# Strassen products for the FFN up projections of a two-layer decoder step, and a down projection in groups of four tiles

## The chip, the core and the metric

The kernel runs on one core of a Trainium2 chip. The metric is device time in microseconds: the median of three runs was 2255.38 us (2253.37 to 2259.19). One more execution was profiled; its time was 2256.28 us and the span of its trace, from the first to the last instruction, 2254.5 us. Engines are named as in the profile: PE (matmul), PEld (the weight load before each matmul), DVE (VectorE), ACT (ScalarE), POOL (GpSimd) and SP (whose queue issues the weight DMAs).

## The reference

One step of two layers over 512 prompt tokens and 32 sample tokens (544 columns in all), model width 1024. A layer has a half-step FFN, a mixing part (state-space heads and windowed attention), a second half-step FFN and a gated input embedding:

```
def _swiglu(x, w1, w3, w2):
    return (jax.nn.silu(x @ w1) * (x @ w3)) @ w2
...
    h = h + (0.5 * _swiglu(_rmsnorm(h, lp['g_ffn1']), lp['w1_a'], lp['w3_a'], lp['w2_a'])).astype(hd)
    ... mixing ...
    h = h + (0.5 * _swiglu(_rmsnorm(h, lp['g_ffn2']), lp['w1_b'], lp['w3_b'], lp['w2_b'])).astype(hd)
    gate = jax.nn.sigmoid(_rmsnorm(h, lp['g_ple']) @ lp['w_ple_gate'])
    h = h + (gate * (pe.astype(hd) @ lp['w_ple_proj'])).astype(hd)
```

`w1` and `w3` (the up projections) are 1024 x 2752, `w2` (the down projection) 2752 x 1024, all float32. The FFN runs four times in the step.

## The kernel before

**Numbers in two halves.** Each float32 operand is split into a rounded part and the rest, `wh` and `wl` for weights, `XH` and `XL` for activations. A product takes three matmuls for each 128 x 128 weight block: `wh` with `XH`, `wh` with `XL`, `wl` with `XH` (`terms3`, L103). A matmul has 128 x 128 weights and 272 columns, half of the 544, so that a pair of PSUM banks holds one output tile (`gemm`, L107).

**Weights.** `load_piece` (L89) takes a raw buffer of 8 blocks (128 x 1024 elements), issues its DMA on SP (L92), makes `wh` by a copy on ACT (L95) and `wl` by a subtraction on DVE (L96). `raw`, `wh` and `wl` have three buffers each (pool `wp`, L45).

**FFN** (L219 to L297). The 2752 hidden units are 21 tiles of 128 and a remainder of 64. For each tile j, `xtile` computes `w1`'s product (8 blocks x 3 terms x 2 halves = 48 matmuls), `act` (L229) takes it out of PSUM, scaled by the norm's factor `Rb` (two DVE instructions, L127), and forms SiLU by a tanh on ACT (L233), a DVE step (L234) and a POOL multiplication (L235); then `w3`'s product takes 48 matmuls, is multiplied in (L271, two DVE instructions) and kept as `UH` (ACT, L272) and `UL` (DVE, L273). After 11 tiles the down projection over these 11 is done for each of the eight 128-row tiles m of `h` and added into `h` (L296); then the other ten tiles and the remainder follow with their own down projection. One down tile over both parts is 130 matmuls. In the second FFN of a layer, `early` (L267) issues `ple_prep` (L1012: two DMAs, ten transposes, four ACT copies, four DVE subtractions) after the second tile, for the embedding stage that follows.

**What sets the order.** The kernel is written as one program; a planner at build time gives each engine its list of instructions. It prefers what stands earlier in the program, but puts a later instruction first where it expects the earlier one not to be ready, and it reuses a buffer of a pool only behind the last reader of what was in it. On the chip each engine works through its list strictly in order. Pools that are opened later lie over the memory of closed ones and wait tile by tile (`reuse_waits="tile"`).

**Elsewhere.** `mix` (L300) uses `piece` and `load_piece` for `w_in` and `w_out`; a loop written by hand (`fill`) mixes these products with attention and scan work. `Norm` (L130) scales and splits `h` into `XH` and `XL` and sums squares, with POOL adding (L151) and PE summing over rows (L156) and spreading the result (L168, L170).

Of the kernel before, what the change touches and what calls it, by code (L numbers as in the profile page):

```python
# [9 lines left out]
F32 = mybir.dt.float32  # L10
F32R = mybir.dt.float32r
# [10 lines left out]
NS = NB * NT  # L22
N = NP + NS
HN = N // 2
KD = DM // 128
DFF = 2752
NJ = DFF // 128
# [11 lines left out]
def hymba_step(ctx: ExitStack, tc: tile.TileContext, I, O):  # L39
# [2 lines left out]

    base = ctx.enter_context(tc.tile_pool(name="base", bufs=1))
    prm_p = ctx.enter_context(tc.tile_pool(name="prm", bufs=2))
    wp = ctx.enter_context(tc.tile_pool(name="wp", bufs=3))  # L45
    nrm = ctx.enter_context(tc.tile_pool(name="nrm", bufs=2))
    psp = ctx.enter_context(tc.tile_pool(name="ps", bufs=8, space=PSUM))

# [37 lines left out]
    V.memset(mhalf, -0.5)  # L86


    def load_piece(parts, nk):  # L89
        raw = wp.tile([128, KD, 128], F32, tag="raw", name="raw")  # L90
        for dst, src in parts:
            nc.sync.dma_start(out=dst(raw), in_=src)  # L92
        wh = wp.tile([128, KD, 128], F32R, tag="wh", name="wh")
        wl = wp.tile([128, KD, 128], F32R, tag="wl", name="wl")
        A.copy(wh[:, 0:nk, :], raw[:, 0:nk, :])  # L95
        V.tensor_sub(wl[:, 0:nk, :], raw[:, 0:nk, :], wh[:, 0:nk, :].bitcast(F32))  # L96
        return wh, wl

    def piece(w, r0, c0, nk):
        src = w[r0:r0 + nk * 128, c0:c0 + 128].rearrange("(k p) m -> p k m", p=128)  # L100
        return load_piece([(lambda t: t[:, 0:nk, :], src)], nk)

    def terms3(wp_, k, xh, xl):  # L103
        wh, wl = wp_
        return [(wh[:, k, :], xh), (wh[:, k, :], xl), (wl[:, k, :], xh)]

    def gemm(groups):  # L107
# [105 lines left out]
                 dtb=b4[:, 1, :], sink=b4[:, 2, :], dsk=dsk, srow=srow)  # L213


    HA = 11
    NWK = 6

    def ffn(g, w1, w3, w2, begun=None, early=None):  # L219
        if begun:  # L220
            first, norm = begun
        else:
            first = (piece(w1, 0, 0, KD), piece(w3, 0, 0, KD))
            norm = Norm(g)
        with tc.tile_pool(name="ffn", bufs=2, reuse_waits="tile") as fp:
            UH = fp.tile([128, HA, N], F32R, tag="UH", name="UH", bufs=1)
            UL = fp.tile([128, HA, N], F32R, tag="UL", name="UL", bufs=1)

            def act(ps1, np_=128):  # L229
                t1 = fp.tile([128, N], F32, tag="t1", name="t1")  # L230
                evac_r(t1, ps1, np_)
                th = fp.tile([128, N], F32, tag="th", name="th")
                A.activation(th[0:np_, :], t1[0:np_, :], AF.Tanh, scale=0.5)  # L233
                V.scalar_tensor_tensor(th[0:np_, :], th[0:np_, :], 1.0, t1[0:np_, :], op0=ALU.add, op1=ALU.mult)  # L234
                G.tensor_tensor(th[0:np_, :], th[0:np_, :], Rb[0:np_, :], op=ALU.mult)  # L235
                return th

            for j0, j1, rem in ((0, HA, False), (HA, NJ, True)):
                for j in range(j0, j1):
                    if rem and j == j1 - 1:  # L240
                        c0 = NJ * 128
                        ps = xgemm(load_piece(
                            [(lambda t: t[:, :, 0:FREM], w1[:, c0:DFF].rearrange("(k p) m -> p k m", p=128)),
                             (lambda t: t[:, :, FREM:128], w3[:, c0:DFF].rearrange("(k p) m -> p k m", p=128))], KD))
                        b = fp.tile([64, N], F32, tag="u64", name="b64", bufs=1)
                        for a in range(2):
                            A.copy(b[:, HALF[a]], ps[a][64:128, 0:HN])
                        s = act(ps, 64)
                        u = fp.tile([128, N], F32, tag="t1", name="ur")
                        V.tensor_tensor(u[0:64, :], b, s[0:64, :], op=ALU.mult)  # L250
                        A.copy(UH[0:64, j1 - j0, :], u[0:64, :])
                        V.tensor_sub(UH[64:128, j1 - j0, :], u[0:64, :], UH[0:64, j1 - j0, :].bitcast(F32))
                    if j == 0:
                        p1 = xgemm(first[0])
                        if not begun:
                            norm.sums()
                        p3 = xgemm(first[1])
                        if begun:
                            norm.sums()
                            pn = xtile(w1, 128)  # L260
                        norm.spread()
                        s = act(p1)
                    else:
                        p1 = pn if begun and j == 1 else xtile(w1, j * 128)
                        s = act(p1)
                        p3 = xtile(w3, j * 128)
                    if j == 1 and early:  # L267
                        early()
                    u = fp.tile([128, N], F32, tag="t1", name="u")
                    for a in range(2):  # L270
                        V.tensor_tensor(u[:, HALF[a]], p3[a][:, 0:HN], s[:, HALF[a]], op=ALU.mult)  # L271
                    A.copy(UH[:, j - j0, :], u)  # L272
                    V.tensor_sub(UL[:, j - j0, :], u, UH[:, j - j0, :].bitcast(F32))  # L273
                nk = j1 - j0
                for m in range(KD):
                    groups = []
                    k0 = 0
                    cuts = [6, nk - 6]
                    for ci, kn in enumerate(cuts):
                        r0 = (j0 + k0) * 128  # L280
                        cs = slice(m * 128, (m + 1) * 128)
                        parts = [(lambda t, kn=kn: t[:, 0:kn, :],
                                  w2[r0:r0 + kn * 128, cs].rearrange("(k p) m -> p k m", p=128))]
                        last = rem and ci == len(cuts) - 1
                        if last:
                            for a in range(2):
                                parts.append((lambda t, kn=kn, a=a: t[a * 64:(a + 1) * 64, kn, :], w2[NJ * 128:DFF, cs]))
                        p = load_piece(parts, kn + int(last))
                        terms = [t for k in range(kn) for t in terms3(p, k, UH[:, k0 + k, :], UL[:, k0 + k, :])]
                        if last:  # L290
                            terms += [(p[0][:, kn, :], UH[:, nk, :]), (p[1][:, kn, :], UH[:, nk, :])]
                        groups.append(terms)
                        k0 += kn
                    ps = gemm(groups)
                    for a in range(2):
                        V.scalar_tensor_tensor(h[:, m, HALF[a]], ps[a][:, 0:HN], 0.25, h[:, m, HALF[a]],  # L296
                                               op0=ALU.mult, op1=ALU.add)  # L297


    def mix(l, P):  # L300
# [3 lines left out]
        with tc.tile_pool(name="mx", bufs=1, reuse_waits="tile") as mp:  # L304
# [271 lines left out]
            rows = mp.tile([64, 168], F32R, tag="rows", name="rows")  # L576

            def step_load():
                raw = wp.tile([128, KD, 128], F32, tag="raw", name="raw")
                nc.sync.dma_start(out=raw, in_=w_in[:, C_DT:C_DT + 128].rearrange("(k p) m -> p k m", p=128))  # L580
                wh = wp.tile([128, KD, 128], F32R, tag="wh", name="wh")
                A.copy(wh, raw)
                V.tensor_sub(wh[:, :, NH:2 * NH], raw[:, :, 0:NH], wh[:, :, 0:NH].bitcast(F32))
                return wh

            def step_gemm(wh):
                ps = gemm([[t for k in range(KD) for t in ((wh[:, k, :], XH[:, k, :]), (wh[:, k, :], XL[:, k, :]))]])
                S["dtf"] = dtf = wk()[:, 0:640]
                evac_r(dtf, ps, 2 * NH)
                G.tensor_copy(dtf[0:2 * NH, NP + NS:640].rearrange("p (a s) -> p a s", s=NS), bc(dtf[0:2 * NH, NP:NP + NS], 1, 3))  # L590
# [290 lines left out]
            def wo_load(part, m):  # L881
                cs = slice(m * 128, (m + 1) * 128)
                if part == 1:
                    return piece(w_out, 0, m * 128, 4)
                return load_piece([(lambda t, a=a: t[a * 64:(a + 1) * 64, 0:4, :],
                                    w_out[512 + a * 256:512 + (a + 1) * 256, cs].rearrange("(j p) m -> p j m", p=64))
                                   for a in range(2)], 4)

# [212 lines left out]
    for l in range(DEPTH):  # L1101
# [5 lines left out]
            V.tensor_copy(selr, sel[:, NH:NH + 4])  # L1107
        mix_params(l, P)
        mix(l, P)
        with tc.tile_pool(name="ple", bufs=2, reuse_waits="tile") as lp:  # L1110
            E = []
            ffn(P["g2"], I["w1_b"][l], I["w3_b"][l], I["w2_b"][l], early=lambda: E.extend(ple_prep(l, lp)))
            Pn = params(l + 1) if l + 1 < DEPTH else None
            ple(l, P, lp, E, l == DEPTH - 1)
        P = Pn
# [64 lines left out]
```

## Time and profile before

| what | value |
| --- | --- |
| median of three runs | 2255.38 us |
| profiled execution | 2256.28 us, of which the span is 2254.5 us |
| mean granted PE clock | 0.989 |
| ACT busy | 699.2 us (31%) |
| POOL busy | 379.8 us (17%) |
| bytes moved by DMA | 197.74 MB, mean 88 GB/s |
| weight loads of 512 KB for `w1`, `w3` | 84 for each of `in_w_a` and `in_w_b` |

Times are in microseconds unless marked ns. In the views by windows, each engine has its busy time in that stretch and, in brackets, its instructions; then come the PE clock as a share of full speed, the share of DMA and GB/s. In the timelines a row has its start, its length, engine, line, operation, output and inputs, and in square brackets the idle time before it with what ended that. In the view of groups by form a row has the total busy time, then the mean of one in ns. Matmuls are pipelined: one lasts about 290 ns in the record, but the next begins after less than half of that, so PE time is counted from start to start. Rows on DVE and ACT overlap their neighbours a little in the same way.

### The profile page before, as it was taken

Reading aid. Unit: us, or ns where it says so; the run is one execution under the profiler, and the core shown is the slowest. Engines: PE = TensorE matmul, PEld = TensorE weight load, DVE = VectorE, ACT = ScalarE, POOL = GpSimd, SP = SyncE. Lnnn points to the kernel's source line nnn. Section 1 sums busy time; section 2 is a strip of 40 time slices with the busy share of each in tenths; the row PEclk is TensorE's granted clock in tenths of the full one; section 3 lists DMA queues with packets and bytes.
Section 4 is the critical chain, followed back from the end, with each engine's and each line's share of the span. In section 5 each row is a group of like instructions: output and inputs, shape, how many; then the busy total and the mean of one; then the engine's idle time right before and its main releaser. Section 6 shows DMA issues by size and latency. Waiting matters only on the chain.

```text
span 2254.5 us, 41580 instructions
## 1 busy us (share of the span) xinstructions
PE 2221.2 (99%) x17666; PEld 2186.0 (97%) x17666; DVE 1161.2 (52%) x2064; ACT 699.2 (31%) x1126; POOL 379.8 (17%) x361
## 2 busy tenths in 40 slices
PE   8999999999999999999999999999999999999999
PEld 8999999989899999999999999999898999999998
DVE  5443444489774434444554334444988644344444
ACT  4221223344342222233432222233443432122333
POOL 3000111233521100101111001112334211001110
PEclk9999999999999999999999999999998999999999
DMA  6323332322243323322333233233123432233223
GB/s 174 99 74 105 85 82 84 92 68 57 65 133 83 88 77 98 93 72 88 96 86 91 72 102 93 72 100 77 50 62 85 125 85 82 79 104 87 78 80 87
DMA packets 396357, 197.74 MB, mean 88 GB/s; under 512 B 35438, under 2 KB 395526, under 8 KB 396172
## 3 DMA queue, kind: packets, MB, share of 16 engines
q1 hardware_dynamic: 394588, 194.91, 31.4%
q8 instruction: 138, 2.26, 0.4%
q14 instruction: 47, 0.39, 0.1%
q10 hardware_dynamic: 1584, 0.18, 0.1%
HBM read 187.56 MB, written 9.53 MB: 87 GB/s over the span
## 4 chain that ended last, share of the span: by engine, by line
PE 91%; DVE 5%; ACT 1%; POOL 1%; issue 1%; DMA 1%; ACTq 0%; POOLq 0%; DVEq 0%
PE ps L113 85%; DVE CV L556 1%; DVE wl L96 1%; PE ps L801 1%; DVE wk L419 1%; POOL acc L151 0%; PE ps L324 0%; DVE am L422 0%; DVE CV L826 0%; PE ps L691 0%; PE ps L156 0%; PE ps L450 0%; PE ps L168 0%; ACT wk L433 0%; PE ps L795 0%
## 5 line engine op out<-in xcount | busy, mean ns | idle before, releaser
L113 PE MATMUL ps<-XH,wh 128*128 128x272 f32 x3744 | 1087.3, 291 | 7.2 <-ACT wk L444 4.8
L113 PE MATMUL ps<-XL,wh 128*128 128x272 f32 x3744 | 1080.7, 289 | 3.0 <-DVE XL L142 2.9
L113 PE MATMUL ps<-XH,wl 128*128 128x272 f32 x3712 | 1073.1, 289 | 0.0
L95 ACT CAST wh<-raw 128x1024 fp32r<-128x1024 f32 (+4 forms) x400 | 361.8, 905 | 1267.5 <-issue 726.7
L113 PEld LDWEIGHTS ps<-XH,wh 128*128 128x128 f32 x3744 | 707.3, 189 | 12.3 <-ACT wk L444 5.2
L113 PEld LDWEIGHTS ps<-XL,wh 128*128 128x128 f32 x3744 | 708.6, 189 | 4.4 <-DVE XL L142 3.6
L113 PEld LDWEIGHTS ps<-XH,wl 128*128 128x128 f32 x3712 | 702.7, 189 | 0.0
L96 DVE TENSOR_TENSOR wl<-raw,wh 128x1024 fp32r<-128x1024 f32 (+4 forms) x400 | 425.9, 1065 | 346.5 <-ACT wh L95 344.5
L113 PE MATMUL ps<-UH,wh 128*128 128x272 f32 x1408 | 402.7, 288 | 0.0
L113 PE MATMUL ps<-UH,wl 128*128 128x272 f32 x1408 | 402.2, 287 | 0.0
L113 PE MATMUL ps<-UL,wh 128*128 128x272 f32 x1344 | 386.2, 287 | 0.0
L235 POOL TENSOR_TENSOR th<-th,Rb 128x544 f32<-128x544 f32 (+1 forms) x88 | 120.6, 1371 | 1148.5 <-DVE th L234 1143.9
L113 PEld LDWEIGHTS ps<-UH,wh 128*128 128x128 f32 x1408 | 265.3, 188 | 0.0
L113 PEld LDWEIGHTS ps<-UH,wl 128*128 128x128 f32 x1408 | 265.3, 188 | 0.0
L113 PEld LDWEIGHTS ps<-UL,wh 128*128 128x128 f32 x1344 | 253.4, 189 | 0.0
L271 DVE TENSOR_TENSOR u<-ps,th 128x272 f32<-128x272 f32 x168 | 73.8, 442 | 222.1 <-POOL th L235 127.6
L127 DVE TENSOR_TENSOR t<-ps,Rb 128x272 f32<-128x272 f32 (+1 forms) x176 | 77.0, 440 | 203.8 <-PE ps L113 189.3
L151 POOL TENSOR_TENSOR acc<-acc,sq 128x544 f32<-128x544 f32 x49 | 76.7, 1565 | 305.0 <-ACT sq L150 304.6
L296 DVE SCALAR_TENSOR_TENSOR h<-ps,h 128x272 f32<-128x272 f32 x128 | 56.5, 442 | 107.4 <-PE ps L113 107.4
L234 DVE SCALAR_TENSOR_TENSOR th<-th,t 128x544 f32<-128x544 f32 (+1 forms) x88 | 63.3, 719 | 7.1 <-ACT th L233 6.8
L233 ACT ACTIVATE th<-t 128x544 f32<-128x544 f32 (+1 forms) x88 | 57.7, 656 | 17.5 <-DVE t L127 17.4
L272 ACT CAST UH<-u 128x544 fp32r<-128x544 f32 x84 | 54.2, 645 | 25.8 <-DVE u L271 25.8
(339 smaller groups left out, 1701.7 us busy)
## 6 DMA issues: line engine op xcount, KB each, us to landing
raw<-in_w_a SPq DMA_DIRECT2D x84, 512.0 KB
raw<-in_w_b SPq DMA_DIRECT2D x84, 512.0 KB
raw<-in_w_in SPq DMA_DIRECT2D x30, 512.0 KB
raw<-in_w_a SPq DMA_DIRECT2D x32, 384.0 KB
raw<-in_w_b SPq DMA_DIRECT2D x32, 384.0 KB
raw<-in_w_ple_gate SPq DMA_DIRECT2D x16, 512.0 KB
raw<-in_w_a SPq DMA_DIRECT2D x16, 320.0 KB
raw<-in_w_a SPq DMA_DIRECT2D x20, 256.0 KB
```

Source lines behind the costliest of these rows:

```text
L95: A.copy(wh[:, 0:nk, :], raw[:, 0:nk, :])
L96: V.tensor_sub(wl[:, 0:nk, :], raw[:, 0:nk, :], wh[:, 0:nk, :].bitcast(F32))
L113: PE.matmul(ps[a][:, 0:HN], lhsT, rhs[:, a * HN:(a + 1) * HN], start=gi == 0 and i == 0, stop=gi == n - 1 and i == len(terms) - 1)
L127: V.tensor_tensor(dst[0:np_, HALF[a]], ps[a][0:np_, 0:HN], Rb[0:np_, HALF[a]], op=ALU.mult)
L151: add.tensor_tensor(self.acc, self.acc, sq, op=ALU.add)
L233: A.activation(th[0:np_, :], t1[0:np_, :], AF.Tanh, scale=0.5)
L234: V.scalar_tensor_tensor(th[0:np_, :], th[0:np_, :], 1.0, t1[0:np_, :], op0=ALU.add, op1=ALU.mult)
L235: G.tensor_tensor(th[0:np_, :], th[0:np_, :], Rb[0:np_, :], op=ALU.mult)
L271: V.tensor_tensor(u[:, HALF[a]], p3[a][:, 0:HN], s[:, HALF[a]], op=ALU.mult)
L272: A.copy(UH[:, j - j0, :], u)
L296: V.scalar_tensor_tensor(h[:, m, HALF[a]], ps[a][:, 0:HN], 0.25, h[:, m, HALF[a]], op0=ALU.mult, op1=ALU.add)
L419: V.scalar_tensor_tensor(P3[:, kv, q, k0:256], sc[kv][:, q * 256:q * 256 + nk], rq[j][:, i, kv:kv + 1], bias_p[:, k0:256], op0=ALU.mult, o ...
```

## The change

Four things change.

**Up projections.** For 20 of the 21 tiles j, the pair (`w1` tile j, `w3` tile j) is taken as a 2 x 2 block matrix (`w1`, `w3` by the two halves of the 1024 inputs) that meets a 2 x 2 block matrix of the activations (the two halves of the inputs by the two halves of the columns). Strassen's scheme in Winograd's form gives the four output blocks from seven block products where eight were needed. A block product is 4 weight blocks x 3 terms = 12 matmuls of 272 columns, as before; a pair has 84. Sums of weight blocks are formed for each pair on POOL (two additions) and DVE (two), and there are seven units to split (`split`: ACT copy and DVE subtraction of 128 x 512). The sums of activation blocks are formed once for each FFN (`block_sums`) and kept in a tile `T`, one of them in place of a quarter of `XH`, `XL`. The outputs are put together on the way out of PSUM: one ACT copy and six DVE instructions, and one more POOL multiplication. Tile 0 and the remainder are still computed plainly (`plain`).

**Down projection.** It is done in groups of four tiles (`PH = 4`); two of the eight down tiles of the group before are issued after each pair of the next group. While the first four pairs run, it is tile 0 and the remainder (`plain_down`, 10 matmuls for an m); later 24 matmuls for an m.

**Weight buffers.** `raw`, `wh`, `wl` become half as large (4 blocks, `KU = 4`) and twice as many (6); `load_piece` loads and splits in units of four blocks everywhere, so also in the mixing and embedding stages. The block sums have buffers of their own: `ra` (raw blocks of `w1`, two), `qh` and `ql` (split sums, two each), `q1` (two).

**`ple_prep`** is issued behind the second FFN.

The core of the diff:

```
-            UH = fp.tile([128, HA, N], F32R, tag="UH", name="UH", bufs=1)
-            UL = fp.tile([128, HA, N], F32R, tag="UL", name="UL", bufs=1)
+            T = fp.tile([128, 6, KU, HN], F32R, tag="T", name="T", bufs=1)
...
+            def block_sums():
+                Y = fp.tile([128, KD, N], F32, tag="U", name="Y")
+                for c in range(KD):
+                    A.activation(Y[:, c, :], h[:, c, :], AF.Copy, scale=g[:, c:c + 1])
+                y11, y12 = Y[:, 0:KU, 0:HN], Y[:, 0:KU, HN:N]
+                y21, y22 = Y[:, KU:KD, 0:HN], Y[:, KU:KD, HN:N]
+                V.tensor_sub(y11, y11, y12)
+                V.tensor_sub(y12, y12, y22)
+                V.tensor_tensor(y22, y22, y11, op=ALU.add)
+                V.tensor_sub(y21, y21, y22)
+                out = []
+                for y, hi, lo in ((y22, T[:, 0], T[:, 1]), (y12, T[:, 2], T[:, 3]),
+                                  (y11, XH[:, 0:KU, HN:N], XL[:, 0:KU, HN:N]), (y21, T[:, 4], T[:, 5])):
+                    A.copy(hi, y)
+                    V.tensor_sub(lo, y, hi.bitcast(F32))
+                    out.append((hi, lo))
+                return out
...
+                a11 = unit(w1, 0, fp, "ra")
+                a21, a22 = unit(w3, 0, wp, "raw"), unit(w3, 1, wp, "raw")
+                a12 = unit(w1, 1, fp, "ra")
+                f11 = split(a11)
+                q1 = fp.tile([128, KU, 128], F32, tag="q1", name="q1")
+                G.tensor_tensor(q1, a21, a22, op=ALU.add)
+                G.tensor_tensor(a21, a21, a11, op=ALU.add)
+                V.tensor_tensor(a11, a11, q1, op=ALU.add)
+                g2 = split(a11, KU, fp, "q")
+                g3 = split(a21, KU, fp, "q")
+                g1 = split(q1, KU, fp, "q")
+                f12 = split(a12)
+                V.tensor_tensor(a12, a12, a11, op=ALU.add)
+                f22 = split(a22)
+                g4 = split(a12, KU, fp, "q")
...
+                prod(pa, f11, x11, True)
+                A.copy(v[:, 0, :], pa[:, 0:HN])
+                prod(pb, g2, t2, True)
+                V.tensor_sub(v[:, 0, :], v[:, 0, :], pb[:, 0:HN])
+                prod(pc, g3, t3, True)
+                V.tensor_sub(v[:, 1, :], v[:, 0, :], pc[:, 0:HN])
+                prod(pd, g1, t1, True)
+                V.tensor_tensor(c2[:, HALF[1]], v[:, 1, :], pd[:, 0:HN], op=ALU.add)
+                prod(pa, f12, x21, False)
+                V.tensor_tensor(t[:, HALF[0]], pa[:, 0:HN], Rb[:, HALF[0]], op=ALU.mult)
+                prod(pc, f22, t4, False)
+                V.tensor_sub(c2[:, HALF[0]], v[:, 0, :], pc[:, 0:HN])
+                prod(pd, g4, x22, False)
+                V.tensor_tensor(t[:, HALF[1]], v[:, 0, :], pd[:, 0:HN], op=ALU.add)
+                G.tensor_tensor(t[:, HALF[1]], t[:, HALF[1]], Rb[:, HALF[1]], op=ALU.mult)
+                th = gated(t)
+                V.tensor_tensor(c2, c2, th, op=ALU.mult)
+                keep(U, i, c2)
...
+            U, sums = plain()
+            last = lambda m, U=U: plain_down(U, m)
+            for j0 in range(1, NJ, PH):
+                U = uset()
+                for i in range(PH):
+                    pair(j0 + i, sums, U, i)
+                    for m in range(2 * i, 2 * i + 2):
+                        last(m)
+                last = lambda m, U=U, j0=j0: down(j0, U, m)
+            for m in range(KD):
+                last(m)
```

`gated` is the tanh, DVE and POOL step of the old `act`; `keep` is the old pair of `UH` copy and `UL` subtraction. In the prediction M1 to M7 are the seven `prod` calls in the order above, and D a down tile.

More of the change, by code (lines that the diff above doesn't have):

```diff
@@ L24 @@
 HN = N // 2
+KU = 4
 KD = DM // 128
@@ L44, in hymba_step @@
     prm_p = ctx.enter_context(tc.tile_pool(name="prm", bufs=2))
-    wp = ctx.enter_context(tc.tile_pool(name="wp", bufs=3))
+    wp = ctx.enter_context(tc.tile_pool(name="wp", bufs=6))
     nrm = ctx.enter_context(tc.tile_pool(name="nrm", bufs=2))
@@ L86, in hymba_step, with raw_unit, split, raw_units @@
     V.memset(mhalf, -0.5)
-    def load_piece(parts, nk):
[L90 to L97, printed above, removed]
+    def raw_unit(loads, pool=wp, tag="raw"):
+        raw = pool.tile([128, KU, 128], F32, tag=tag, name=tag)
+        for dst, src in loads:
+            nc.sync.dma_start(out=dst(raw), in_=src)
+        return raw
+    def split(raw, n=KU, pool=wp, tag="w"):
+        wh = pool.tile([128, KU, 128], F32R, tag=tag + "h", name=tag + "h")
+        wl = pool.tile([128, KU, 128], F32R, tag=tag + "l", name=tag + "l")
+        A.copy(wh[:, 0:n, :], raw[:, 0:n, :])
+        V.tensor_sub(wl[:, 0:n, :], raw[:, 0:n, :], wh[:, 0:n, :].bitcast(F32))
+        return wh, wl
+    def raw_units(parts, nk):
+        return [raw_unit([(lambda t, dst=dst: dst(t)[:, 0:min(KU, nk - k0), :], src[:, k0:min(k0 + KU, nk), :])
+                          for dst, src in parts]) for k0 in range(0, nk, KU)]
+    def load_piece(parts, nk):
+        return [split(raw, min(KU, nk - i * KU)) for i, raw in enumerate(raw_units(parts, nk))]
     def piece(w, r0, c0, nk):
         src = w[r0:r0 + nk * 128, c0:c0 + 128].rearrange("(k p) m -> p k m", p=128)
-        return load_piece([(lambda t: t[:, 0:nk, :], src)], nk)
-    def terms3(wp_, k, xh, xl):
-        wh, wl = wp_
+        return load_piece([(lambda t: t, src)], nk)
+    def terms3(p, k, xh, xl):
+        wh, wl = p[k // KU]
+        k %= KU
         return [(wh[:, k, :], xh), (wh[:, k, :], xl), (wl[:, k, :], xh)]
@@ L213, in mix_params, with ffn @@
                  dtb=b4[:, 1, :], sink=b4[:, 2, :], dsk=dsk, srow=srow)
-    HA = 11
     NWK = 6
-    def ffn(g, w1, w3, w2, begun=None, early=None):
+    PH = 4
+    def ffn(g, w1, w3, w2, begun=None):
         if begun:
@@ L225, in ffn, with uset, gated @@
         with tc.tile_pool(name="ffn", bufs=2, reuse_waits="tile") as fp:
-            UH = fp.tile([128, HA, N], F32R, tag="UH", name="UH", bufs=1)
-            UL = fp.tile([128, HA, N], F32R, tag="UL", name="UL", bufs=1)
-            def act(ps1, np_=128):
-                t1 = fp.tile([128, N], F32, tag="t1", name="t1")
-                evac_r(t1, ps1, np_)
+            T = fp.tile([128, 6, KU, HN], F32R, tag="T", name="T", bufs=1)
+            def uset():
+                return fp.tile([128, 2, PH, N], F32R, tag="U", name="U")
+            def gated(t1, np_=128):
                 th = fp.tile([128, N], F32, tag="th", name="th")
@@ L236, in act @@
                 return th
[L238 to L297, printed above, removed]
@@ new lines, in act, with keep @@
+            def act(ps1, np_=128):
+                t1 = fp.tile([128, N], F32, tag="t1", name="t1")
+                evac_r(t1, ps1, np_)
+                return gated(t1, np_)
+            def keep(U, i, u):
+                A.copy(U[:, 0, i, :], u)
+                V.tensor_sub(U[:, 1, i, :], u, U[:, 0, i, :].bitcast(F32))
+            def block_sums():
[15 more added lines that the diff above has]
+                return out
@@ new lines, in plain @@
+            def plain():
+                U = uset()
+                p1 = xgemm(first[0])
+                if not begun:
+                    norm.sums()
+                p3 = xgemm(first[1])
+                if begun:
+                    norm.sums()
+                else:
+                    norm.spread()
+                c0 = NJ * 128
+                ps = xgemm(load_piece(
+                    [(lambda t: t[:, :, 0:FREM], w1[:, c0:DFF].rearrange("(k p) m -> p k m", p=128)),
+                     (lambda t: t[:, :, FREM:128], w3[:, c0:DFF].rearrange("(k p) m -> p k m", p=128))], KD))
+                if begun:
+                    norm.spread()
+                sums = block_sums()
+                s = act(p1)
+                u = fp.tile([128, N], F32, tag="c2", name="u")
+                for a in range(2):
+                    V.tensor_tensor(u[:, HALF[a]], p3[a][:, 0:HN], s[:, HALF[a]], op=ALU.mult)
+                keep(U, 0, u)
+                b = fp.tile([64, N], F32, tag="c2", name="b64")
+                for a in range(2):
+                    A.copy(b[:, HALF[a]], ps[a][64:128, 0:HN])
+                s = act(ps, 64)
+                u = fp.tile([64, N], F32, tag="c2", name="ur")
+                V.tensor_tensor(u, b, s[0:64, :], op=ALU.mult)
+                A.copy(U[0:64, 0, 1, :], u)
+                V.tensor_sub(U[64:128, 0, 1, :], u, U[0:64, 0, 1, :].bitcast(F32))
+                return U, sums
@@ new lines, in plain_down @@
+            def plain_down(U, m):
+                cs = slice(m * 128, (m + 1) * 128)
+                parts = [(lambda t: t[:, 0, :], w2[0:128, cs])]
+                parts += [(lambda t, a=a: t[a * 64:(a + 1) * 64, 1, :], w2[NJ * 128:DFF, cs]) for a in range(2)]
+                p = split(raw_unit(parts), 2)
+                terms = terms3([p], 0, U[:, 0, 0, :], U[:, 1, 0, :])
+                terms += [(p[i][:, 1, :], U[:, 0, 1, :]) for i in range(2)]
+                add_down(m, gemm([terms]), 0.25)
@@ new lines, in add_down, with pair, unit, prod @@
+            def add_down(m, ps, f):
+                for a in range(2):
+                    V.scalar_tensor_tensor(h[:, m, HALF[a]], ps[a][:, 0:HN], f, h[:, m, HALF[a]], op0=ALU.mult, op1=ALU.add)
+            def pair(j, sums, U, i):
+                def unit(w, k, pool, tag):
+                    src = w[k * 512:(k + 1) * 512, j * 128:(j + 1) * 128].rearrange("(k p) m -> p k m", p=128)
+                    return raw_unit([(lambda t: t, src)], pool, tag)
+                a11 = unit(w1, 0, fp, "ra")
[13 more added lines that the diff above has]
+                g4 = split(a12, KU, fp, "q")
+                t2, t3, t1, t4 = sums
+                x11, x21, x22 = ((XH[:, k:k + KU, c:c + HN], XL[:, k:k + KU, c:c + HN]) for k, c in ((0, 0), (KU, 0), (KU, HN)))
+                def prod(ps, f, x, start):
+                    for k in range(KU):
+                        for n, (lhsT, rhs) in enumerate(terms3([f], k, x[0][:, k, :], x[1][:, k, :])):
+                            PE.matmul(ps[:, 0:HN], lhsT, rhs, start=start and k == 0 and n == 0, stop=k == KU - 1 and n == 2,
+                                      skip_group_check=not start)
+                pa, pb, pc, pd = bank(), bank(), bank(), bank()
+                v = fp.tile([128, 2, HN], F32, tag="v", name="v")
+                t = fp.tile([128, N], F32, tag="t1", name="t")
+                c2 = fp.tile([128, N], F32, tag="c2", name="c2")
+                prod(pa, f11, x11, True)
[16 more added lines that the diff above has]
+                keep(U, i, c2)
@@ new lines, in down @@
+            def down(j0, U, m):
+                src = w2[j0 * 128:(j0 + PH) * 128, m * 128:(m + 1) * 128].rearrange("(k p) m -> p k m", p=128)
+                p = load_piece([(lambda t: t, src)], PH)
+                add_down(m, gemm([[t for k in range(PH) for t in terms3(p, k, U[:, 0, k, :], U[:, 1, k, :])]]), -0.25)
+            U, sums = plain()
+            last = lambda m, U=U: plain_down(U, m)
+            for j0 in range(1, NJ, PH):
+                U = uset()
+                for i in range(PH):
[3 more added lines that the diff above has]
+                last = lambda m, U=U, j0=j0: down(j0, U, m)
@@ L578, in step_load @@
             def step_load():
[L579 to L584, printed above, removed]
+                out = []
+                for raw in raw_units([(lambda t: t, w_in[:, C_DT:C_DT + 128].rearrange("(k p) m -> p k m", p=128))], KD):
+                    wh = wp.tile([128, KU, 128], F32R, tag="wh", name="wh")
+                    A.copy(wh, raw)
+                    V.tensor_sub(wh[:, :, NH:2 * NH], raw[:, :, 0:NH], wh[:, :, 0:NH].bitcast(F32))
+                    out.append(wh)
+                return out
             def step_gemm(wh):
-                ps = gemm([[t for k in range(KD) for t in ((wh[:, k, :], XH[:, k, :]), (wh[:, k, :], XL[:, k, :]))]])
+                ps = gemm([[(wh[k // KU][:, k % KU, :], x[:, k, :]) for k in range(KD) for x in (XH, XL)]])
                 S["dtf"] = dtf = wk()[:, 0:640]
@@ L884, in wo_load @@
                     return piece(w_out, 0, m * 128, 4)
-                return load_piece([(lambda t, a=a: t[a * 64:(a + 1) * 64, 0:4, :],
+                return load_piece([(lambda t, a=a: t[a * 64:(a + 1) * 64],
                                     w_out[512 + a * 256:512 + (a + 1) * 256, cs].rearrange("(j p) m -> p j m", p=64))
@@ L1109, in hymba_step @@
         mix(l, P)
+        ffn(P["g2"], I["w1_b"][l], I["w3_b"][l], I["w2_b"][l])
         with tc.tile_pool(name="ple", bufs=2, reuse_waits="tile") as lp:
-            E = []
-            ffn(P["g2"], I["w1_b"][l], I["w3_b"][l], I["w2_b"][l], early=lambda: E.extend(ple_prep(l, lp)))
+            E = ple_prep(l, lp)
             Pn = params(l + 1) if l + 1 < DEPTH else None
```

## The prediction

> **What bounds the kernel now.** I read the page's head first, then windows over the first and the last of the four FFNs, then the chain that ended last.
>
> ```profile
> span 2254.5 us, 41580 instructions
> PE 2221.2 (99%) x17666; PEld 2186.0 (97%) x17666; DVE 1161.2 (52%) x2064; ACT 699.2 (31%) x1126; POOL 379.8 (17%) x361
> ```
> ```profile
> 29.00:410.00 381.00, 380.66 (x3018) 380.28 (x3018) 165.62 (x251) 101.70 (x135) 42.14 (x33) 1.00 0.34 93
> 1815.00:2184.00 369.00, 369.00 (x2938) 368.79 (x2938) 158.49 (x236) 100.05 (x135) 36.90 (x26) 1.00 0.31 86
> ```
> ```profile
> 38.10 371.99 PE ps L113 x2960
> ```
>
> The first and the last FFN's windows show PE without a gap at full clock, DVE busy 43%, ACT 27%, POOL 11%. The chain runs on PE alone through 2960 matmuls in 371.99 us, 0.1257 us each. So the FFN costs what its matmuls cost, and everything else hides. Fewer matmuls gain time until another engine becomes late.
>
> **Matmuls taken away.** Before, an FFN has 21 x 96 + 48 = 2064 up matmuls and 8 x 130 = 1040 down matmuls, 3104. After, 3 x 48 = 144 plain ones, 20 pairs of 84 = 1680, and the same 1040: 2864. That is 240 fewer, 960 over four FFNs, 960 x 0.1257 = 120.6 us. Shape and columns are unchanged, so I keep 0.1257. This gain is the upper end; what follows eats from it.
>
> A pair with its two D now takes PE (84 + 48) x 0.1257 = 16.6 us; in the first group, whose D are the short ones, (84 + 20) x 0.1257 = 13.1 us. There are 16 and 4 of these per FFN.
>
> **DVE, ACT and POOL per pair.** The durations, from the groups by form, then two timelines:
>
> ```profile
> L96 DVE TENSOR_TENSOR wl<-raw,wh 128x1024 fp32r<-128x1024 f32 x224 | 277.4, 1239 | 136.3 <-ACT wh L95 136.2
> L235 POOL TENSOR_TENSOR th<-th,Rb 128x544 f32<-128x544 f32 x84 | 115.2, 1371 | 1102.8 <-DVE th L234 1098.2 <-PE ps L113 4.6
> L127 DVE TENSOR_TENSOR t<-ps,Rb 128x272 f32<-128x272 f32 x168 | 73.6, 440 | 201.6 <-PE ps L113 189.3 <-ACT Rb L171 3.8
> L273 DVE TENSOR_TENSOR UL<-u,UH 128x544 fp32r<-128x544 f32 x84 | 60.4, 719 | 3.0 <-ACT UH L272 3.0
> L233 ACT ACTIVATE th<-t 128x544 f32<-128x544 f32 x84 | 55.1, 655 | 12.9 <-DVE t L127 12.8
> L95 ACT CAST wh<-raw 128x512 fp32r<-128x512 f32 x32 | 19.9, 621 | 61.8 <-PE ps L113 61.5
> L96 DVE TENSOR_TENSOR wl<-raw,wh 128x256 fp32r<-128x256 f32 x16 | 6.8, 423 | 4.1 <-ACT wh L95 4.1
> ```
> ```profile
> 105.71 1.23 DVE L96 TENSOR_TENSOR wl<-raw,wh 128x1024 fp32r<-128x1024 f32 x1 [0.56 <-ACT wh L95]
> 106.85 0.72 DVE L273 TENSOR_TENSOR UL<-u,UH 128x544 fp32r<-128x544 f32 x1
> ...
> 658.84 0.69 DVE L96 TENSOR_TENSOR wl<-raw,wh 128x512 fp32r<-128x512 f32 x1
> ```
> ```profile
> 584.61 1.28 POOL L678 TENSOR_TENSOR wk<-wk,CBm 128x512 f32<-128x512 f32 x1
> ```
>
> The first two timeline rows show that neighbours overlap: the second starts 1.14 us after a row of 1.23. So I take 0.08 off each DVE row when they are queued: 0.61 for 128x512, 0.34 for 128x256, 0.36 for a 272-column read of PSUM, 0.64 for 128x544.
>
> DVE, a full pair: seven splits, two sums and two D splits, 11 x 0.61 = 6.7; six output steps and four D additions, 10 x 0.36 = 3.6; three steps of 544 columns, 1.9. Together 12.2 us against 16.6 on PE. In the first group the two D splits are 0.34: 9 x 0.61 + 0.7 + 3.6 + 1.9 = 11.7 against 13.1. Before, a tile had 2 x 1.15 + 4 x 0.36 + 2 x 0.64 = 5.0 against 96 x 0.1257 = 12.1. So DVE goes from idle most of the time to 74%, and 89% in the first group.
>
> ACT: nine copies of 0.62, one tanh 0.66, one keep about the same, one PSUM copy (I put it at a DVE read, 0.44): 7.3 of 16.6, covered. POOL: two sums of 1.28, half of 1.37 for 272 columns, 1.37: 4.6 us, little by itself.
>
> **DVE and POOL together.** The trace of before holds POOL and DVE apart in the FFN (DVE waits for POOL's product), but the stage before the second FFN shows them side by side:
>
> ```profile
> 659.58 0.79 DVE L142 SCALAR_TENSOR_TENSOR XL<-h,pg,XH 128x544 fp32r<-128x544 f32 x1
> ...
> 663.79 1.75 DVE L142 SCALAR_TENSOR_TENSOR XL<-h,pg,XH 128x544 fp32r<-128x544 f32 x1
> ```
> ```profile
> 663.60 1.36 POOL L151 TENSOR_TENSOR acc<-acc,sq 128x544 f32<-128x544 f32 x1 [2.02 <-ACT sq L150]
> ```
>
> The same DVE instruction takes 0.79 alone and 1.75 when it meets a running POOL addition: it ends 0.58 after POOL's end, at 665.54, as if it had stood still until POOL was done. All splits, sums and 544-column steps have two SBUF inputs like this one; the ten PSUM readers of a pair (3.6 us) do not, and I let them pass. The Trainium skill, page "SBUF — State Buffer", section "Who interferes with whom", says it as a rule: a VectorE instruction with two SBUF inputs and a GpSimd instruction that reads SBUF exclude each other, and the later one waits for the whole of the earlier. The rows agree; by the rule, taken to its end, the sum would be the serial bound of the next paragraph.
>
> Bounds: if POOL's 4.6 us all falls into DVE's idle time, nothing is lost. If none does, a full pair needs 12.2 + 4.6 = 16.8 of DVE, 0.2 over PE, and a first-group pair 11.7 + 4.6 = 16.3, 3.2 over: per FFN 16 x 0.2 + 4 x 3.2 = 16.0 us. I take for the first group 11.7 + 4.6 less 0.2 of each of four POOL instructions that passes beside PSUM readers, 15.5, so 2.4 over: 4 x 2.4 = 9.6, near the serial end, because DVE there has hardly idle time. For the other sixteen, the load is 16.0 of 16.6, just under PE; I take a quarter of a 1.37 us wait per pair reaching PE, 0.34: 5.4 us. Together 15.0.
>
> **The beginning of an FFN.** `block_sums` adds eight DVE instructions of 1088 elements (1239 ns x 1088/1024 - 0.08 = 1.24 each, 9.9 us), eight ACT scalings of about 0.66 and four copies of 1088 (two of 0.62 each at most, 5.0): 10.2 us. The stage as it is:
>
> ```profile
> 678.43 6.22 PE ps L113 x48
> 684.65 0.89 PE ps L168 x8
> ...
> 685.87 12.25 PE ps L113 x96
> 698.13 0.44 PE ps L1023 x4
> 698.56 0.18 PE ps L1025
> 698.74 0.59 PE ps L1023 x4
> 699.33 0.17 PE ps L1025
> ```
> ```profile
> 669.92:699.50 29.58, 29.58 (x221) 28.97 (x221) 13.79 (x23) 9.12 (x13) 4.91 (x4) 0.94 0.28 76
> ```
>
> DVE is busy 13.8 of 29.6 us here. With 9.9 more and a pair's prepared weights in place of a tile's (9 x 0.61 less 2 x 1.15, 3.2) it has 26.9: it fits, tightly, under three plain products. The first sum must be there one product after them. Two sums also wait, since one overwrites a quarter of `XH` after the remainder's product has read it; two products (M2, M3: 3.0 us) cover its copy and subtraction (about 2.4). I take 2 us per FFN, between 0 and 6, what one late sum with its subtraction and the weight splits queued behind it costs.
>
> **Moves and halves.** `ple_prep`'s ten transposes (0.44 + 0.18 + 0.59 + 0.17 = 1.4 us) stay on PE; behind the FFN its two DMAs (544 KB, 5.8 us at the 93 GB/s of the first window) and transposes are covered by the last eight D, 192 x 0.1257 = 24 us, since its buffers should lie where `T` was (both pools open at the same place), which the last pair frees; on SP they pass only weight loads that are issued ahead. Without that cover it would cost 7 us a layer. The last pair's way from M7 to the kept `U` (0.44 + 0.69 + 0.66 + 0.72 + 1.37 + 0.72 + 0.66 + 0.72 = 6.0) is covered by the two D behind it, 6.0, and by nine matmuls on the other three tiles. Half-sized pieces cost two starts on DVE (2 x 0.61 against 1.15, 0.07 a piece) and save half a piece where PE waits for one; zero, give or take 2 us a layer. Each is at nothing in the sum.
>
> **Sum.** 4 x (15.0 + 2) = 68; 2256.3 - 120.6 + 68 = 2203.7, and 0.9 less for the median of the runs: 2203.
>
> **Rivals.** *PE stays fed.* Then only the head's 2 us per FFN remain: 2256.3 - 120.6 + 8 - 0.9 = 2143. For it speaks that the planner breaks a product up where its next step is not ready:
>
> ```profile
> 1560.25 1.09 PE ps L113 x7
> 1561.34 1.26 PE ps L414 x8
> 1562.60 7.78 PE ps L113 x41
> ```
>
> Seven matmuls, eight others, then the 41 left: M5, M6 or D can fill a hole in a pair. Against it speaks that DVE has 1.4 us to spare in a first-group pair while POOL takes 4.6.
>
> *No gain measurable.* The stalls happen to come to about 30 us per FFN: 2255.
>
> *Slower: the two buffers for split sums.* There are four such units in a pair and two buffers. g1's split may begin only when M2 is through with g2, and M4 needs it one product later. How long the turn takes:
>
> ```profile
> 109.78 0.28 PE L113 MATMUL ps<-XH,wh 128*128 128x272 f32 x1
> ```
> ```profile
> 110.73 0.44 DVE L127 TENSOR_TENSOR t<-ps,Rb 128x272 f32<-128x272 f32 x1 [2.58 <-PE ps L113]
> ```
>
> At 109.78 PE goes to the other bank, and the idle DVE reads the finished one at 110.73: 0.95 us. With the copy (0.62) and the subtraction (0.69) that is 2.26 from M2's end, M3 covers 12 x 0.1257 = 1.51: 0.75 late. Alone, 80 x 0.75 = 60 us, still a gain. With a POOL instruction of 1.37 standing before the subtraction it is 2.12, 170 us: 2256.3 - 120.6 + 170 - 0.9 = 2305. It decides from 120.6/80 = 1.5 us a pair. Against it: M5 doesn't need g1 and can go first. A second price may come on top, since PE after a pause is slower:
>
> ```profile
> 505.51 0.40 PE L113 MATMUL ps<-XH,wh 128*128 128x272 f32 x1 [2.37 <-ACT wk L444]
> ...
> 506.55 0.43 PE L113 MATMUL ps<-XL,wh 128*128 128x272 f32 x1
> 506.78 0.43 PE L113 MATMUL ps<-XH,wl 128*128 128x272 f32 x1
> ```
>
> Behind 2.37 us of idle, matmuls start 0.23 apart. Pauses of 0.75 would hardly do that, one of 2.1 could.
>
> That the change has other products than it says isn't open: the counts follow from the loops.
>
> **How the numbers follow.** Forecast 0.46 (2203, own range 2160 to 2245); PE stays fed 0.24; no gain 0.07; the buffers 0.23, spread from 2262 to 2305. A measurement tells apart about 0.3%, 6.8 us. Faster 0.46 + 0.24 = 0.70, same 0.07, slower 0.23. The range goes from 2140, under which 0.06 lies, to 2275, over which 0.14 lies.
>
> **What would show it.** Right: 16,706 matmuls, FFN windows with PE some 95% busy, DVE near 85%, gaps of PE released by DVE, widest in the first group, and DVE splits of 0.69 stretched to about 1.5 beside POOL. Wrong: gaps released by ACT or DMA, pauses of over 2 us with a clock under 1.00 in the FFN windows, DVE rows unstretched beside POOL, or the gap at the head over 6 us.

## The result and the profile after

The changed kernel takes 2348.03 us (median of four runs, 2343.03 to 2351.44) where the kernel before takes 2255.24: a ratio of 1.041, 95% interval 1.038 to 1.043. It is slower, by 92.8 us, and outside the predicted range. Its profiled execution took 2343.03 us, with a span of 2341.2.

The page's head of the changed kernel, the lines that answer to those shown of before:

```profile
span 2341.2 us, 43271 instructions
PE 2165.0 (92%) x16706; PEld 2102.5 (90%) x16706; DVE 1801.2 (77%) x3282; ACT 938.6 (40%) x1784; POOL 711.7 (30%) x601
```

The 960 matmuls are gone (17666 less 16706), and yet the span is longer: PE stands still for 176 us, 33 before. The windows over the four FFNs of the changed kernel (length, then busy time of PE, PEld, DVE, ACT and POOL, PE clock, DMA share, GB/s):

```profile
29.00:444.00 415.00, 370.24 (x2791) 362.20 (x2792) 321.71 (x545) 157.32 (x284) 129.33 (x92) 0.97 0.32 87
706.00:1115.00 409.00, 379.88 (x2882) 373.61 (x2882) 325.29 (x542) 159.34 (x285) 118.94 (x88) 0.97 0.30 83
1200.00:1594.00 394.00, 365.91 (x2771) 358.75 (x2772) 319.94 (x531) 153.34 (x275) 116.80 (x85) 0.97 0.32 86
1856.00:2261.00 405.00, 376.03 (x2883) 369.61 (x2882) 323.19 (x543) 160.09 (x287) 120.49 (x87) 0.98 0.30 84
```

I added up PE's start-to-start times in these windows beyond 0.1257 us a matmul. Intervals of over 0.5 us, the pauses, give 144 us for the four FFNs, and intervals of about 0.23, nearly twice the usual, another 48; in the kernel before, the windows over its four FFNs give about 2 for both. That is where the gain went: 144 + 48 against 120.6. About 13 us more lie at the two embedding stages.

Most of it is one pause, again and again. PE's timeline in a steady pair, and PE's waits over the whole span (in all, times, longest):

```profile
278.02 0.32 PE L354 MATMUL ps<-XH,qh 128*128 128x272 f32 x1
278.18 0.29 PE L354 MATMUL ps<-XL,qh 128*128 128x272 f32 x1
280.01 0.39 PE L354 MATMUL ps<-XH,ql 128*128 128x272 f32 x1 [1.54 <-DVE ql L101]
```
```profile
PE ps L354 <- DVE ql L101: 91.1, 71, 2.3
```

These are the first three matmuls of M4: `qh` is there, `ql`, the subtraction of g1's split, is not. It is the place that the slower rival named. In this pair M1 to M4 take 7.89 us with the pause (273.49 to 281.38), M5 to M7 and the two D 10.52 without one (281.38 to 291.90): 18.4 us where PE has work for 16.6. The same count over all pairs, from each pair's first matmul to that of the next and less 0.1257 us a matmul, gives 129 us lost in the 60 full pairs that have a successor in their FFN, 2.1 each, and 62 us in the sixteen first-group pairs, where the pauses are rarer and longer.

Who made `ql` late is not PE. The chain of waits over one turn, in order of time (start, length, what), small pieces left out:

```profile
281.91 2.91 DMA ra<-in_w_a
284.84 0.63 ACT wh L100
285.49 0.69 DVE wl L101
...
286.45 0.70 DVE ra L345
...
287.20 2.96 DMA ra<-in_w_a
...
290.29 1.63 POOL raw L339
291.92 1.78 POOL th L250
...
293.72 0.74 DVE c L377
...
296.24 0.61 DVE wl L101
...
298.43 0.43 DVE v L366
...
300.45 2.86 DMA ra<-in_w_a
```

From one load of `ra` to the same load a turn later are 18.54 us, and no PE instruction is in it. Read it as a ring. A raw buffer for `a12` is given back when g4's split has read it; the next `a12` loads (2.91), is split, and is added to (L345), which gives `a11`'s buffer back; the next `a11` loads (2.96); POOL adds it into `a21` (L339); the tanh product (L250) stands behind that in POOL's list, DVE waits for that product (L377), and in DVE's list behind it stand f11's and g1's subtractions and at last g4's, which gives a buffer back. Each engine keeps its own order; together they close, and g1's subtraction, which M4 needs, comes only when the turn reaches it.

The last link is drawn out by POOL. DVE and POOL at 280 us:

```profile
279.27 0.69 DVE L101 TENSOR_TENSOR ql<-q,qh 128x512 fp32r<-128x512 f32 x1
...
280.22 1.66 DVE L101 TENSOR_TENSOR ql<-ra,qh 128x512 fp32r<-128x512 f32 x1
...
282.15 0.68 DVE L101 TENSOR_TENSOR ql<-ra,qh 128x512 fp32r<-128x512 f32 x1
```
```profile
280.03 1.30 POOL L338 TENSOR_TENSOR q<-raw 128x512 f32<-128x512 f32 x1 [4.91 <-DVE ql L101]
```

The `ql` at 279.27 frees a buffer of `q1`, POOL's next sum begins at once, and the next subtraction takes 1.66 in place of 0.68. The Trainium skill, page "SBUF — State Buffer", section "Who interferes with whom", says that a VectorE instruction with two SBUF inputs and a GpSimd instruction that reads SBUF exclude each other, so that the later one waits for the whole of the earlier. These rows agree: the sum ends at 281.33, the subtraction at 281.88.

### The profile page after: what moved, and what is told of

It is laid out like the page before. It is cut to its first block, busy times and chain, and to the rows that moved or that the text cites. A ratio compares the mean times of both kernels' runs of the same rounds, so it can differ in the third digit from the quotient of the medians.

```text
span 2341.2 us, 43271 instructions
## 1 busy us (share of the span) xinstructions
PE 2165.0 (92%) x16706; PEld 2102.5 (90%) x16706; DVE 1801.2 (77%) x3282; ACT 938.6 (40%) x1784; POOL 711.7 (30%) x601
## 4 chain that ended last, share of the span: by engine, by line
PE 35%; DVE 24%; DMA 15%; issue 11%; POOL 9%; ACT 4%; SPq 0%; POOLq 0%; ACTq 0%; DVEq 0%
PE ps L126 21%; PE ps L354 9%; DMA ra<-in_w_b 7%; DMA ra<-in_w_a 6%; DVE wl L101 6%; POOL th L250 5%; POOL raw L339 4%; DVE c L377 2%; DVE ra L345 2%; ACT wh L100 2%; DVE ql L101 2%; DVE CV L654 2%; ACT U L259 1%; DVE h L325 1%; DVE v L364 1%
## 5 line engine op out<-in xcount | busy, mean ns | idle before, releaser
L126 PE MATMUL ps<-U,wh 128*128 128x272 f32 x2752 | 523.7, 288 | 0.0
L126 PEld LDWEIGHTS ps<-U,wh 128*128 128x128 f32 x2752 | 432.8, 188 | 0.0
L101 DVE TENSOR_TENSOR wl<-raw,wh 128x512 fp32r<-128x512 f32 (+1 forms) x448 | 368.6, 826 | 71.3 <-ACT wh L100 65.1
L126 PE MATMUL ps<-U,wl 128*128 128x272 f32 x1408 | 401.0, 287 | 0.0
L126 PE MATMUL ps<-XH,wh 128*128 128x272 f32 x1184 | 349.7, 298 | 8.9 <-DVE wk L517 4.3
L126 PE MATMUL ps<-XL,wh 128*128 128x272 f32 x1184 | 343.5, 292 | 2.3 <-DVE XL L155 2.2
L126 PE MATMUL ps<-XH,wl 128*128 128x272 f32 x1152 | 335.1, 291 | 0.0
L126 PEld LDWEIGHTS ps<-XH,wh 128*128 128x128 f32 x1184 | 225.5, 191 | 14.4 <-DVE wk L517 4.7
L126 PEld LDWEIGHTS ps<-XL,wh 128*128 128x128 f32 x1184 | 226.6, 192 | 3.8 <-DVE XL L155 3.4
L126 PEld LDWEIGHTS ps<-XH,wl 128*128 128x128 f32 x1152 | 220.4, 191 | 0.0
L354 PE MATMUL ps<-XH,wh 128*128 128x272 f32 x640 | 192.9, 301 | 11.9 <-ACT wh L100 10.6
L354 PE MATMUL ps<-XH,wl 128*128 128x272 f32 x640 | 191.8, 300 | 0.9 <-DVE wl L101 0.9
```

Of the source, the lines that this page charges most:

```text
L101: V.tensor_sub(wl[:, 0:n, :], raw[:, 0:n, :], wh[:, 0:n, :].bitcast(F32))
L126: PE.matmul(ps[a][:, 0:HN], lhsT, rhs[:, a * HN:(a + 1) * HN], start=gi == 0 and i == 0, stop=gi == n - 1 and i == len(terms) - 1)
L354: PE.matmul(ps[:, 0:HN], lhsT, rhs, start=start and k == 0 and n == 0, stop=k == KU - 1 and n == 2, skip_group_check=not start)
```

## The experiments

Four theories stood. **A**, the rival of the prediction: sums are split into two recycled buffers, and g1 waits for M2. **B**: the ring above. **C**: DVE, with POOL on its path, is simply full. And for the first group, whose pairs have less PE work, C by itself ("theory 1" below), against loads or the way from PSUM to the kept tile ("theory 2"). Ratios are to the kernel before on the same chip. The steady stretch from 180 to 400 us of each kernel, in windows, serves as a common measure: without a pause PE does 220/0.1257 = 1750 matmuls in it. The changed kernel:

```profile
180.00:400.00 220.00, 201.42 (x1570) 197.97 (x1570) 172.08 (x287) 78.51 (x144) 67.39 (x47) 1.00 0.31 85
```

**Four buffers for the split sums.**

```
-        wh = pool.tile([128, KU, 128], F32R, tag=tag + "h", name=tag + "h")
+        wh = pool.tile([128, KU, 128], F32R, tag=tag + "h", name=tag + "h", bufs=4 if tag == "q" else None)
```

(and the same for `wl`)

> Base: 2348 us, 18.45 us a pair in the steady part, of which PE works 16.6 and stands still 1.7 at the third matmul of M4 (it waits for g1's subtraction). Theory A (split sums recycle two buffers: g1's split waits for M2 to be through): with four buffers g1 is split ahead, the 1.7 us go in some 64 pairs, 109 us and part of the 48 us at half clock with them: 2200 to 2245. Theory B (two raw buffers for w1: the chain of waits closes a ring through two 2.9 us loads, POOL's additions and DVE, without PE): the ring still lasts 18.5 us, 2348 give or take 15. Theory C (DVE with POOL on the same port is simply full): 2348 give or take 30.

Measured 2256.11 us, ratio 1.000 (0.999 to 1.001). The steady stretch:

```profile
180.00:400.00 220.00, 219.57 (x1737) 218.36 (x1736) 181.12 (x313) 88.49 (x154) 65.76 (x49) 1.00 0.33 91
```

The pause is all but gone; 92 us less than the changed kernel, 11 us short of A's range. B as it was stated, 2348 with the ring untouched, missed here.

**Four raw buffers.**

```
-        raw = pool.tile([128, KU, 128], F32, tag=tag, name=tag)
+        raw = pool.tile([128, KU, 128], F32, tag=tag, name=tag, bufs=4 if tag == "ra" else None)
```

> Four raw buffers for w1's blocks in place of two. Theory A: g1 still waits for M2, 2348 give or take 15, the pause at M4 stays at about 1.7. Theory B: the loads leave the ring, a pair falls to 16.6 to 17.2, 2230 to 2265. Theory C: 2348 give or take 30.

Measured 2266.14, ratio 1.004 (1.003 to 1.006), 1 us above B's range; and the pause at M4, which A says stays, is all but gone here too, though g1 still has two buffers. What is left of it is 0.15 us in three pairs, and a pair takes 17.0 us:

```profile
180.00:400.00 220.00, 218.39 (x1716) 215.78 (x1716) 189.33 (x308) 91.10 (x152) 59.80 (x48) 1.00 0.33 90
```

**Both.**

> Four buffers for the split sums and four raw ones. Theory A: as with the split sums alone, 2200 to 2245. Theory B: as with the raw ones alone, 2230 to 2265. If the two are limits behind each other, only this one falls, to about 2200. Theory C: 2348 give or take 30.

Measured 2240.95, ratio 0.993 (0.991 to 0.995): a little faster than before. The steady stretch has no pause at all, with DVE at 85%; what is still lost lies in the first-group pairs (53 us by the count above) and the first full pairs behind them (29):

```profile
180.00:400.00 220.00, 220.00 (x1755) 220.00 (x1754) 187.69 (x313) 93.67 (x157) 60.71 (x48) 1.00 0.34 92
```

So C falls for the steady part: with all the work of the change, DVE keeps up.

**M5 before M4**, no buffers added.

```
+                prod(pa, f12, x21, False)
+                V.tensor_tensor(t[:, HALF[0]], pa[:, 0:HN], Rb[:, HALF[0]], op=ALU.mult)
                 prod(pd, g1, t1, True)
                 V.tensor_tensor(c2[:, HALF[1]], v[:, 1, :], pd[:, 0:HN], op=ALU.add)
-                prod(pa, f12, x21, False)
-                V.tensor_tensor(t[:, HALF[0]], pa[:, 0:HN], Rb[:, HALF[0]], op=ALU.mult)
```

> No buffers added; M5 stands before M4 in the program, so that g1's turn has two products (3.0 us) in place of one as cover. Theory A: 1.5 of the 1.7 us go, 2348 - 96 = 2252, unless M7, which adds to M4's bank, waits instead. Theory B: the ring is untouched, 2348 give or take 15. Theory C: 2348 give or take 30.

Measured 2335.31, ratio 1.035 (1.033 to 1.037), 13 us less than the change as it is. A said 96. The pause only moves and splits in two, before M5 (0.7 to 0.9) and at M4 (0.57), and a pair still takes 18.5 us (from 257.79 to 276.27). M5 adds to M1's bank, and waits for ACT's copy of M1 out of it; that copy stands on ACT behind the copy of the kept tile (L259), which waits for L377 of the ring:

```profile
257.79 0.39 PE L354 MATMUL ps<-XH,wh 128*128 128x272 f32 x1 [0.74 <-ACT v L362]
```
```profile
180.00:400.00 220.00, 203.13 (x1568) 197.87 (x1567) 170.93 (x288) 77.60 (x144) 66.75 (x47) 1.00 0.30 85
```

That is B's mark: covering one wait of a ring with PE work frees little, and more buffers at either of the two places tried open it. A's buffers are a link of the ring, which B had left out. In the changed kernel the copy of g4's split waits for M3 of its own pair, and `a12`'s raw buffer comes back at 281.88, 8.4 us after that pair's M1 began. With four split buffers it waits for M7 of the pair before, and the raw buffer comes back 4.0 us before M1 (277.15 against 281.18 in that trace).

**POOL's sums left out, with two and two buffers.**

```
-                q1 = fp.tile([128, KU, 128], F32, tag="q1", name="q1")
-                G.tensor_tensor(q1, a21, a22, op=ALU.add)
-                G.tensor_tensor(a21, a21, a11, op=ALU.add)
+                q1 = a22
```

> The changed kernel with its two and two buffers, without POOL's two sums of weight blocks (g1 splits a22, g3 splits a21 without a11, so the up products are not the reference's). Theory B, a ring through two raw loads, POOL's sums and DVE: without POOL's a21 sum (1.4 to 1.6 us), the tanh product queued behind it and the split that stands still beside the other sum (1.0), the ring is shorter than PE's 16.6, the pauses of the steady part go, 2348 - 118 and some of the first group: 2180 to 2235. Theory A, two split buffers alone: g1 still waits for M2, 0.4 to 0.8 us a pair stay, 2255 to 2290.

Measured 2243.92, ratio 0.994 (0.993 to 0.996). Between the two forecasts:

```profile
180.00:400.00 220.00, 215.68 (x1696) 213.17 (x1695) 176.18 (x305) 85.81 (x154) 31.24 (x26) 1.00 0.34 93
```

The ring loses most of its excess, 104 us in all; pauses of 0.2 to 1.1 us at M4 stay in seven pairs of the stretch. By the count above the full pairs lose 30 us in place of 129. So POOL's two additions are a link as well. What is left of the ring is about as long as PE's work: behind the longest of these pauses, at 304.18, the chain of waits runs back for 17 us through DVE's list, the tanh step and a load of `ra`, with no product in it, so it isn't A's wait for M2. The first-group pairs still lose 59 us in place of 62: with two and two buffers POOL's sums are not what limits them.

**POOL's sums left out, with both sets of buffers** (the same edit on the third kernel), for the first group.

> The kernel with both sets of four buffers (2241 us), without POOL's two sums of weight blocks: g1 splits a22 itself and g3 splits a21 without a11, so the up products are not the reference's; everything else runs as it did. Theory 1, DVE with POOL in its way sets the first group (15.3 to 15.6 us a pair there, PE's work 13.1): DVE's 11.7 and POOL's remaining 2.1 give 13.3 to 13.8 a pair, 16 pairs, 2206 to 2216. Theory 2, the first group is set by loads or by the way from PSUM to the kept tile: 2241 give or take 8.

Measured 2180.19, ratio 0.966 (0.964 to 0.968): 61 us less than with the sums, more than forecast. Two first-group pairs of the second FFN with the sums, and one without:

```profile
734.80:750.10 15.30, 13.63 (x104) 13.20 (x104) 13.52 (x25) 5.55 (x12) 5.43 (x4) 1.00 0.42 121
750.10:765.70 15.60, 13.67 (x105) 13.23 (x105) 13.81 (x25) 6.61 (x13) 6.56 (x4) 1.00 0.36 102
```
```profile
730.70:744.70 14.00, 13.41 (x105) 13.19 (x105) 12.22 (x25) 6.60 (x13) 2.45 (x2) 1.00 0.42 114
```

These two pairs go from 15.3 and 15.6 us to about 14.0. They are not the whole of it: the sixteen first-group pairs average 16.4 us with the sums (13.1 to 20.9) and 14.3 without. By the count above their loss falls from 53 to 20 us, and that of the full pairs behind them from 29 to 4: 58 of the 61. Theory 2 falls; with the buffers open, POOL's sums are the main cost of the first group.

**Half-sized weight units alone**, on the kernel before (`load_piece` in units of four blocks, six buffers).

> The kernel before with weight units of four blocks, six buffers, in all stages (down pieces of 4, 4 and 3 blocks in place of 6 and 5), and nothing else of the change. The prediction put these at nothing: 2257 give or take 5. Rival: the additional starts on DVE and ACT show, 2262 to 2275.

Measured 2258.01, ratio 1.000 (0.999 to 1.001). They cost nothing.

**A plain first group.** Its four tiles are computed with `xtile` as before, the other sixteen pairs by block sums; three raw and three split buffers.

```
+            def classic(j, sums, U, i):
+                s = act(xtile(w1, j * 128))
+                p3 = xtile(w3, j * 128)
...
+                keep(U, i, u)
...
-                    pair(j0 + i, sums, U, i)
+                    (classic if j0 == 1 else pair)(j0 + i, sums, U, i)
```

> The first group of four tiles is computed plainly (96 matmuls a tile), the other sixteen pairs by block sums, with three raw and three split buffers and one v buffer (the memory holds no more; the fourth activation sum has a place of its own). 768 fewer matmuls than before in place of 960. If DVE full in the first group is the cause, a tile there takes PE's 14.6 us in place of 15.5, and the pauses at its beginning and end go: 2241 - 14 - (0 to 15), 2212 to 2227. If the pauses come from elsewhere, the 192 matmuls come back as time: about 2241 + 24 = 2265.

Measured 2198.52, ratio 0.973 (0.971 to 0.976). It has 192 more matmuls (24 us of PE) than with both sets of buffers and takes 42 us less, some 13 us below the forecast range.

**And the embedding's preparation later.**

```
             if m == 0:
                 norm.sums()
+                EH, EL = ple_prep(l, lp)
             p = piece(wpj, 0, m * 128, 2)
```

> As the one before, and the embedding's preparation (loads, transposes) is issued behind the first product of the embedding stage in place of ahead of it. If the pause of 3 us and what follows it at the beginning of that stage come from that step, 2 x 5 to 7 us less than the one before: 2200 to 2217. If the step is covered anyway, no difference.

Measured 2186.00 (2183.28 to 2189.97), ratio 0.968 (0.967 to 0.970): 12.5 us less, and the fastest version that leaves none of the reference's work out. In the changed kernel SP and PE show what this was:

```profile
1110.30 3.38 SPq L94 DMA_DIRECT2D raw<-in_w_ple_gate  x2
1113.72 0.50 SPq L1115 DMA_DIRECT2D pt<-in_p_prompt  x1
```
```profile
1118.05 0.63 PE L1122 MATMUL ps<-ident,pt 128*128 128x128 f32 x4 [3.02 <-DMA pt<-in_p_prompt]
```

The load of `pt` stood on SP behind two weight loads that waited for raw buffers.

**Every second tile of the first group plain.**

> The version with a plain first group and the late embedding step (2186 us), but only every second tile of the first group plain (its result negated, so that the group has one sign). 96 matmuls fewer, 12 us. DVE has about 7 + 15.5 us for two tiles of which PE takes 14.6 + 13.1: if DVE full was the cause in the first group, it fits and 2172 to 2180 comes out; if single block-sum pairs stall there at any rate, 2186 to 2200.

Measured 2194.00 (2191.81 to 2205.40), ratio 0.973 (0.970 to 0.976). Not better than four plain tiles: the 96 matmuls saved come back as pauses at M6, which waits for a PSUM step on DVE (1.9 and 1.7 us in the first FFN). Whether another order would keep them wasn't tried.

## Why the prediction was wrong

**Right.** The matmuls taken away, 960. DVE's sum: in the version with both sets of buffers the steady part runs at PE's 16.6 us a pair with DVE at 85%, as the load of 12.2 and POOL's stalls said. The half-sized units at nothing. Gaps released by DVE and splits stretched to 1.66 beside POOL came as signs of being right; so did a sign of being wrong, pauses of over 2 us with a clock of 0.97 to 0.98 in the FFN windows.

**Right in kind, too small.** The first group: 15.5 us a pair forecast, 38 us in all over PE's work; 62 measured in the changed kernel, and 53 (16.4 a pair) with the ring open. POOL's sums are shown as its main cause there.

**Wrong, and it decided the sign.** The step that failed is "the other sixteen": "a quarter of a 1.37 us wait per pair reaching PE, 0.34". It measured 2.1 us a pair, 129 us where 64 x 0.34 = 22 were forecast. The cost was taken from busy time only, as if a load under PE's were enough. The sum had no term for the turn of a buffer: two raw buffers, each with a load of 2.9 us between two uses, in a loop with instructions of three engines that run in order. A row for that load stood in no step, though the buffers were in the diff.

**The rival.** It named the right instruction and its price, 0.75 to 2.12 us a pair, holds the 1.8 us of the steady pair. Its mechanism was only one link: by it M5 in front should have freed 96 us, and freed 13; and raw buffers alone, which it does not mention, freed 82. Its own total, 2305 at most, is 43 us short of the measured one: the pairs lost 191 us in place of its 170, the embedding stages 13 more, and the rest isn't separated. I gave it 0.23 because PE could fill the hole with M5 or D. The planner did not; each engine's list was fixed and PE waited at M4 71 times.

**Pauses and the clock.** The intervals of 0.23 took 48 us in the FFNs, in no sum of mine for the forecast. About 34 of these are runs of twelve or more behind a pause, where the granted clock is 0.5 for 3.4 or 6.8 us. Most runs lie in the first groups and at the FFNs' beginnings. In the first FFN's steady stretch, with a pause of 1.54 every 18.5 us, none follows, and the row above has a clock of 1.00; but in the steady parts of the other three, six of the same pauses are followed by such a run, as here behind the one that ends at 969.52:

```profile
969.60:973.20 3.60, 3.60 (x17) 3.60 (x18) 2.88 (x4) 0.62 (x1) 1.22 (x1) 0.53 0.14 35
```

Why one pause does it and the next does not stays open. The other 14 us are mostly single intervals beside a pause.

**`ple_prep` at nothing** was wrong too: 12.5 us for two stages. I looked at memory and at PE for its cover, and took SP's queue for free; in it the load stood behind two that waited.

**The head** at 2 us per FFN: not separated. Pauses of 1 to 6 us stand in the changed kernel's first pairs. With both sets of buffers they reach 3.6 us at most, and with POOL's sums left out as well, four of 1.2 to 1.5 us are left in the pairs of the four FFNs.

## What to carry to other kernels

Busy time under the bound engine's work is necessary, not enough: for each buffer that is used again, walk from its release through the load, the engines and what stands ahead in their lists back to the release, and compare that turn with the period. If the chain of waits of a steady stretch holds no instruction of the engine that should be the bound, look for such a ring; more buffers at one place in it freed 82 to 92 us here, a better order on the engine that waits 13. A tight stage at the beginning (here the first group) may be worth keeping in the old, more expensive form.

## What the runs showed of the hardware

A POOL instruction pays too when it meets one of DVE: the multiplication of 128 x 272, put at 0.69 in the prediction, takes 0.77 us with DVE idle and 1.15 when it begins beside a running split (288.00 to 288.68), with a mean of 1.03 us in the changed kernel. The mean mixes the two cases.

```profile
414.19 0.77 POOL L375 TENSOR_TENSOR t<-t,Rb 128x272 f32<-128x272 f32 x1 [12.13 <-DVE t L374]
...
288.16 1.15 POOL L375 TENSOR_TENSOR t<-t,Rb 128x272 f32<-128x272 f32 x1 [6.83 <-DVE t L374]
```
```profile
288.00 0.68 DVE L101 TENSOR_TENSOR ql<-raw,qh 128x512 fp32r<-128x512 f32 x1
```
```profile
L375 POOL TENSOR_TENSOR t<-t,Rb 128x272 f32<-128x272 f32 x80 | 82.0, 1025 | 540.1 <-DVE t L374 540.1
```

And a load of 256 KB takes 2.9 us from issue to landing in the steady part, while the core moves 85 to 92 GB/s there: a delay in a ring, not a lack of bandwidth, since with both sets of buffers the same loads leave PE no pause in the stretch, at 92 GB/s.
